# A planned decoder trunk: new constants in the plan's model of loads and product changes, and two filler products in place of eleven

## The chip, the cores and the metric

The kernel runs on one core of one Trainium2 chip. The metric is the device time of one execution in microseconds (us), the median of several runs. The core has five engines that run their own instruction streams and meet only at semaphores: TensorE (PE, with its weight loads shown as PEld), VectorE (DVE), ScalarE (ACT), GpSimd (POOL) and SyncE (SP, which here does nothing but issue DMAs).

## The reference

The program is a decoder trunk of two layers over a sequence of 512 tokens with 1024 features, all in float32. What one layer computes, cut to its core:

```python
mod = c_silu @ w_ada + b_ada
shift, scale, gate = jnp.split(mod, 3, axis=-1)
u = rms_norm(x, norm_g) * (1 + scale[:, None]) + shift[:, None]
z = u @ w_in                       # 18 column groups: q, k, v, gates of three mixers, indexer, merge gates
ya = dsa_attention(...)     * silu(ag)   # indexer scores, top 128 keys, softmax attention
yb = swa_sinks_attention(...) * silu(bg) # window of 128 keys, sinks
yc = stick_breaking_attention(...) * silu(cg)
merged = sigmoid(ma) * (ya @ w_br_a) + sigmoid(mb) * (yb @ w_br_b) + sigmoid(mc) * (yc @ w_br_c)
x = x + gate[:, None] * (merged @ w_out)
```

After both layers a final `rms_norm` is taken. Each mixer has eight heads of 64 features.

## The kernel before

**Staging.** Activations lie with features on the partitions, as 8 tiles of 128 x 512. Nearly every product is made in three parts: weights and activations are each split into a high part and a low part (`whi`, `wlo`; `uh`, `ul`), and TensorE adds high x high, high x low and low x high in one PSUM bank. Weights come as 128 x 512 pieces through four buffers (`wstage`); a cast makes `whi`, a subtraction makes `wlo`, on whichever of ACT, DVE and POOL the plan picks.

A layer runs through five parts: `first_phase` (L923: seven column tiles over all eight `u` tiles, so that it can begin as soon as `u` tile 0 stands), `v_phase` (L975: the value columns), a long middle in which the three mixers, the remaining column tiles and the branch products are woven together, and `out_phase` (L1360). In the mixers, each pair of heads goes through score products, softmax or stick-breaking on ACT and DVE, 128 x 128 transposes (`softmax_tr`, L1218), and then `softmax_pv` (L1244): eight products whose stationary operand is only 64 columns wide, four key blocks (j) for each of two heads (e), written in the program in the order e0 j0, e1 j0, e0 j1, e1 j1 and so on. The two heads write the two halves of the same PSUM bank. These are the half-width products; the model calls them mode "c". Another sort, mode "r", has only 64 rows (`low_parts`, L1073, seven products in one item). Full products are "m", transposes "t".

**The plan.** No instruction is issued where the program names it. `Recorder.add` (L280) records every operation with its data dependencies and, where several engines could do it, the alternatives. `price` (L313) gives each alternative a cost (how long it holds its engine) and a lag (when its result stands). `forward` (L385) then plays the whole program: at each step it takes, over all engines, the instruction that can start first, and among those that can start at the same time on an engine the one with the most urgent priority. `latest` (L506) works back from the end and gives each instruction the latest time at which it may start; that is the priority of the next round. There are five rounds (L253), the first with program order as priority, and the round with the earliest modelled end is issued (`emit`, L545; every profile row therefore has line L555, or L553 for the seven products of mode "r"). The chip runs each engine's instructions strictly in the order that the plan wrote down, whatever the real times are. The model's times decide only that order, the choice of engine and the choice of buffer.

Loads are modelled as one queue: a DMA lands at `max(at + 1.9, dma_free)` plus its bytes over a rate, and `dma_free` is the landing of the one before. A product costs more when the mode changes from or to "c" or "r".

**The start of the program** (`start`, L1436) is where the second part of the edit lies. It issues eight products on a constant (`WARM`), computes `silu(c)` and spreads it over the partitions (`csr`, two products), loads x in two halves of 256 tokens (`norm`, L1459: loads, squares on ACT, products with a constant that sum over the features, then `rstd_of`: a logarithm and an exponential on ACT). The scale and shift of `u` tile j come from 512 KB loads into `Y` (`ada_load`, L724) and two long multiply-and-sum operations on DVE (`ada_first`, L729). Between these stand filler products: `busy` (L1469) multiplies a constant with the first 128 columns of a tile into a bank that nobody reads, so that a filler waits for its tile and then occupies TensorE.

Of the kernel before, what the change touches and what calls it, by code (L numbers as in the profile page):

```python
# [249 lines left out]
class Recorder:  # L250
# [62 lines left out]
    def price(self, x, engine, op, args, kw):  # L313

        y = Way()
        y.op, y.args, y.kw, y.mode, y.port = op, args, kw, None, False
        o = x.writes[0] if x.writes else None
        if op == "preload_act_table_set":
            y.cost = y.lag = 1.3
            return y  # L320
        if op == "dma_start":
            n = 1
            for d in (o or x.reads[0]).shape:
                n *= d
            y.cost, y.lag, y.mode = 0.35 if engine == "SP" else 0.1, n * 4 / 365e3, "dma"
            return y
        n = 1
        for d in o.shape[1:]:
            n *= d
        from_psum = any(v.tile.pool.name[:3] == "ps_" for v in x.reads)  # L330
        if engine == "PE":
            if op == "pairs":
                w = [q[2].shape[-1] for q in args]
                c, y.mode = 0.095 + sum(max(0.112, 0.4375e-3 * v + 0.007) for v in w[::2]), "r"
                y.cost, y.lag = c, c + self.PIPE
            elif op == "transpose":
                c, y.mode = 0.109, "t"
                y.cost, y.lag = c, c + self.PIPE
            elif args[1].shape[-1] == 64:
                c, y.mode = 4 * n / 2.4e3 / 2 + 0.03, "c"  # L340
                y.cost, y.lag = c, 2 * c + self.PIPE
            else:
                rhs, y.mode = args[2], "m"
                c = 4 * n / 2.4e3 + 0.01 if rhs.dtype == F32 else 0.06 if rhs.dtype == BF16 else 0.4375e-3 * n + 0.007
                y.cost, y.lag = c, c + self.PIPE
            return y
        accum = "accum_out" in kw
        if engine == "ACT":
            b = 0.1 if isinstance(kw.get("bias"), View) or isinstance(kw.get("scale"), View) else 0.0
            c = 0.2 + 0.82e-3 * n + (b if not accum else 0.08) - (0.03 if from_psum else 0)  # L350
        elif engine == "DVE":
            y.port = not from_psum and op not in ("max", "match_replace", "memset", "reciprocal")
            if op == "tensor_tensor_scan":
                c = 1.21
            elif op == "max":
                c = 0.15 + 1.05e-3 * args[1].shape[-1]
            elif op == "match_replace":
                c = 0.145 + 1.05e-3 * args[2].shape[-1]
            elif n <= 16:
                c = 0.2 + (0.1 if accum else 0)  # L360
            elif op == "tensor_tensor_reduce":
                c = 0.147 + 1.05e-3 * n
            elif from_psum:
                c = 0.147 + 1.05e-3 * n + (0.08 if accum else 0)
            elif op in ("tensor_scalar", "tensor_copy"):
                c = 0.2 + 0.45e-3 * n if op == "tensor_scalar" else 0.15 + 0.5e-3 * n
            elif op == "memset":
                c = 0.1 + 0.6e-3 * n
            else:
                c = 0.15 + 1.05e-3 * n + (0.08 if accum else 0)  # L370
        else:
            y.port = n > 16
            if op == "memset":
                c = 0.12 if n < 16 else 0.52
            elif op == "tensor_copy":
                c = 0.2 + 0.82e-3 * n
            elif op == "tensor_scalar":
                c = 0.2 + 2.8e-3 * n
            else:
                c = 0.1 + 2.35e-3 * n  # L380
        y.cost = y.lag = c
        return y


    def forward(self):  # L385
        E = {e: {"free": 0.0, "mode": None, "ready": {}, "pend": []} for e in self.real}
        port = dma_free = 0.0
        waiting = {}
        for x in self.list:
            x.left, x.est, x.bound, x.taken = len(x.preds), 0.0, len(x.tiles), False  # L390
# [8 lines left out]
        def offer(x):  # L399
            if x.left == 0 and x.bound == 0:  # L400
                for e in x.alts:
                    heapq.heappush(E[e]["pend"], (x.est, x.i))
# [20 lines left out]
        while len(out) < len(self.list):  # L423
            best = None
            for name, e in E.items():
                free, pend, ready = e["free"], e["pend"], e["ready"]
                while pend and pend[0][0] <= free + 1e-9:
                    i = heapq.heappop(pend)[1]
                    ready[i] = self.list[i]
                mine = None  # L430
                for i in list(ready):
                    x = ready[i]
                    if x.taken:
                        del ready[i]
                        continue
                    y = x.alts[name]
                    at = max(free, port) if y.port else free
                    if len(x.alts) > 1 and self.elsewhere(x, name, at, E, port):
                        continue
                    key = (at, x.prio, i)  # L440
                    if mine is None or key < mine:
                        mine = key
                if mine is None or mine[0] > free + 1e-9:
                    while pend and self.list[pend[0][1]].taken:
                        heapq.heappop(pend)
                    if pend:
                        est, i = pend[0]
                        x = self.list[i]
                        at = max(est, port) if x.alts[name].port else est
                        key = (at, x.prio, i)  # L450
                        if (mine is None or key < mine) and not (len(x.alts) > 1 and self.elsewhere(x, name, at, E, port)):
                            mine = key
                        elif mine is None:
                            mine = None
                if mine is not None:
                    asked = max(free, self.list[mine[2]].est)
                    if best is None or (mine[0], asked, mine) < best[:3]:
                        best = (mine[0], asked, mine, name)
            assert best is not None, "no instruction may go"
            (at, _, i), name = best[2:]  # L460
            e, x = E[name], self.list[i]
            y = x.alts[name]
            x.taken, x.engine = True, name
            e["ready"].pop(i, None)
            hold = y.cost
            if name == "PE":
                if e["mode"] is not None and y.mode != e["mode"]:
                    hold += 0.095 if {"c", "r"} & {y.mode, e["mode"]} else 0.0
                e["mode"] = y.mode
            x.start, x.hold = at, hold  # L470
            e["free"] = at + hold
            if y.port:
                port = at + hold
            if y.mode == "dma":
                x.end = dma_free = max(at + 1.9, dma_free) + y.lag
            else:
                x.end = at + y.lag + (hold - y.cost)
            out.append(x)
            for s in x.succs:
                s.est = max(s.est, x.end + self.between(x, s))  # L480
                s.left -= 1
                offer(s)
            for t in x.tiles:
                t.users -= 1
                t.done = max(t.done, x.end + self.CROSS)
                if t.users == 0:
                    heapq.heappush(t.pool.free, (t.done, t.slot))
                    give(t.pool)
# [89 lines left out]
def trunk(ctx, tc, xT, vecs, w_ss, w_gt, w_first, w_t, w_v, w_br, w_o, rope, consts, out):  # L578
# [7 lines left out]
    PE, ACT, DVE, POOL, SP = (rec.engine(e) for e in ("PE", "ACT", "DVE", "POOL", "SP"))  # L586

    def fixed(name, shape, dt=F32):
        return rec.fixed(const.tile(shape, dt, name=name))
# [13 lines left out]
    def mm(o, lhsT, rhs, start, stop=True):  # L603
        PE.matmul(o, lhsT, rhs, start=start, stop=stop, skip_group_check=True)
# [831 lines left out]
    def start():  # L1436
# [4 lines left out]
        e = fixed("e", [P, 8], F32)  # L1441
# [14 lines left out]
        x = st["x"] = [xx[k // 4][:, k % 4] for k in range(KT)]  # L1456
# [12 lines left out]
        def busy(n, v):  # L1469
            for _ in range(n):  # L1470
                mm(st["warm"][:, :P], f(nones), v[:, :P], True)
# [1 line left out]
        norm(HALVES[0])  # L1473
        ada_load(0)
        ch.load(1)
        busy(3, ch.raw[0][0])
        busy(4, ch.raw[1][0])
        ada_first(0)
        for k in (0, 1):
            times_rstd(x[k], HALVES[0])  # L1480
            busy(2, x[k])
        make_u(0, 0, x[0], HALVES[0])
        norm(HALVES[1])
        ada_load(1)
# [48 lines left out]
    ch = Chunks(seq)  # L1533
# [72 lines left out]
```

## Time and profile before

| what | us |
|---|---|
| median of three runs (lowest, highest) | 1219.49 (1219.07, 1220.74) |
| the profiled execution | 1219.63 |
| its span, first to last instruction | 1217.8 |
| TensorE busy in the span | 1200.4 |
| VectorE busy | 962.1 |
| ScalarE busy | 556.3 |
| GpSimd busy | 264.3 |

Rows of the profile name an operation by engine, instruction, output and inputs. "xN" counts records: a product with plain float32 operands leaves two records, one with split operands leaves one. In a row of the timeline the first number is the start in us from the span's beginning, the second how long the row lasts, and the bracket gives the engine's idle time before it and what ended that. TensorE products overlap: the time that one takes from the next is the distance between starts, which is shorter than its duration.

### The profile page before, as it was taken

Reading aid. Unit: us, or ns where it says so; the run is one execution under the profiler, and the core shown is the slowest. Engines: PE = TensorE matmul, PEld = TensorE weight load, DVE = VectorE, ACT = ScalarE, POOL = GpSimd, SP = SyncE. Lnnn points to the kernel's source line nnn. Section 1 sums busy time; section 2 is a strip of 40 time slices with the busy share of each in tenths; the row PEclk is TensorE's granted clock in tenths of the full one; section 3 lists DMA queues with packets and bytes.
Section 4 is the critical chain, followed back from the end, with each engine's and each line's share of the span. In section 5 each row is a group of like instructions: output and inputs, shape, how many; then the busy total and the mean of one; then the engine's idle time right before and its main releaser. Section 6 shows DMA issues by size and latency. Waiting matters only on the chain.

```text
span 1217.8 us, 17816 instructions
## 1 busy us (share of the span) xinstructions
PE 1200.4 (99%) x6006; PEld 976.3 (80%) x6006; DVE 962.1 (79%) x2106; ACT 556.3 (46%) x1166; POOL 264.3 (22%) x290
## 2 busy tenths in 40 slices
PE   9999999999999999999999999999999999999997
PEld 8899777788777887688898987777878878877886
DVE  6867999899879888686476699989996887667754
ACT  6623677454445532632143157664534654234222
POOL 1200446432111110011200015454220110100120
PEclk9999999999999999999999999999999999999999
DMA  9644222344334455245533432223442324323343
GB/s 318 231 119 124 83 70 84 104 114 117 109 96 122 129 146 150 69 130 145 171 109 98 133 95 78 85 69 116 121 122 70 96 80 120 95 64 79 93 123 102
DMA packets 81915, 139.40 MB, mean 114 GB/s; under 512 B 10016, under 2 KB 22560, under 8 KB 81824
## 3 DMA queue, kind: packets, MB, share of 16 engines
q1 hardware_dynamic: 80672, 136.17, 38.6%
q10 hardware_dynamic: 1152, 2.10, 0.5%
q8 instruction: 47, 0.77, 0.3%
q14 instruction: 44, 0.36, 0.1%
HBM read 125.39 MB, written 4.19 MB: 106 GB/s over the span
## 4 chain that ended last, share of the span: by engine, by line
PE 89%; DVE 4%; SPq 2%; DMA 2%; ACT 1%; issue 1%; POOL 1%; DVEq 0%; ACTq 0%; POOLq 0%
PE ps_z L555 67%; PE ps_s L555 22%; SPq L555 2%; PE ps_s L553 1%; DMA m<-zs 1%; DVE t L555 1%; DVE Q L555 1%; DVE m L555 1%; DMA wstage<-in_w_first 1%; DMA wstage<-in_w_t 0%; ACT t L555 0%; POOL KH L555 0%; DVE score L555 0%; DVE zc L555 0%; DVE den L555 0%
## 5 line engine op out<-in xcount | busy, mean ns | idle before, releaser
L555 PE MATMUL ps_z<-uh,whi 128*128 128x512 f32 (+1 forms) x908 | 359.1, 397 | 2.2 <-DVE xm L555 2.2
L555 PE MATMUL ps_z<-uh,wlo 128*128 128x512 f32 (+1 forms) x908 | 356.0, 393 | 0.0
L555 PE MATMUL ps_z<-ul,whi 128*128 128x512 f32 (+1 forms) x908 | 355.8, 392 | 0.0
L555 POOL TENSOR_TENSOR wlo<-wstage,whi 128x512 fp32r<-128x512 f32 (+1 forms) x131 | 175.1, 1339 | 662.8 <-DVE whi L555 312.0
L555 PEld LDWEIGHTS ps_z<-uh,whi 128*128 128x128 f32 x908 | 170.3, 188 | 41.9 <-DVE xm L555 3.1
L555 PEld LDWEIGHTS ps_z<-uh,wlo 128*128 128x128 f32 x908 | 170.5, 188 | 38.7 <-issue 1.8
L555 PEld LDWEIGHTS ps_z<-ul,whi 128*128 128x128 f32 x908 | 170.6, 188 | 35.9 <-issue 1.0
L555 DVE TENSOR_TENSOR wlo<-wstage,whi 128x512 fp32r<-128x512 f32 (+2 forms) x241 | 158.2, 660 | 12.8 <-ACT whi L555 3.6
L555 DVE CAST whi<-wstage 128x512 fp32r<-128x512 f32 (+2 forms) x181 | 74.7, 412 | 112.9 <-PE ps_z L555 94.5
L555 ACT CAST whi<-wstage 128x512 fp32r<-128x512 f32 (+2 forms) x141 | 83.4, 596 | 169.7 <-PE ps_z L555 125.9
L555 PE MATMUL ps_z<-Y,whi 128*128 128x512 f32 x384 | 121.7, 396 | 0.0
L555 ACT ACTIVATE e<-ps_z 128x512 f32<-128x512 f32 x68 | 40.2, 592 | 131.7 <-PE ps_z L555 131.4
L555 PEld LDWEIGHTS ps_z<-Y,whi 128*128 128x128 f32 x384 | 71.7, 188 | 17.0
L555 ACT ACTIVATE e<-e 128x512 f32<-128x512 f32 x96 | 60.6, 633 | 39.9 <-DVE e L555 39.1
L555 PE MATMUL ps_z<-Y,wlo 128*128 128x512 f32 x192 | 75.8, 395 | 0.0
L555 ACT ACTIVATE t<-t 128x512 f32<-128x512 f32 x120 | 71.8, 628 | 6.1 <-DVE t L555 2.7
L555 ACT ACTIVATE t<-t,nm 128x256 f32<-128x256 f32 (+3 forms) x128 | 65.2, 511 | 18.0 <-DVE nm L555 17.9
L555 PEld LDWEIGHTS ps_s<-small,t 128*128 128x128 f32 x432 | 50.3, 140 | 13.3 <-ACT t L555 2.9
L555 PE MATMUL ps_s<-small,t 128*128 128x128 f32 x432 | 58.6, 274 | 1.8 <-ACT t L555 1.3
L555 POOL CAST whi<-wstage 128x512 fp32r<-128x512 f32 (+2 forms) x50 | 31.2, 623 | 134.0 <-PE ps_z L555 63.1
L555 DVE SCALAR_TENSOR_TENSOR wstage<-wstage,csr 128x512 f32<-128x512 f32 x64 | 47.3, 740 | 9.4 <-DMA wstage<-in_w_ss 6.7
L555 DVE MAX8 m<-score 128x8 f32<-128x256 f32 (+2 forms) x96 | 53.2, 555 | 1.0
(208 smaller groups left out, 2066.8 us busy)
## 6 DMA issues: line engine op xcount, KB each, us to landing
wstage<-in_w_t SPq DMA_DIRECT2D x212, 256.0 KB, 2.7
wstage<-in_w_v SPq DMA_DIRECT2D x48, 182.0 KB, 2.4
Y<-in_w_ss SPq DMA_DIRECT2D x16, 512.0 KB, 6.7
m<-zs SPq DMA_DIRECT2D x128, 64.0 KB, 2.0
wstage<-in_w_gt SPq DMA_DIRECT2D x32, 256.0 KB, 2.7
wstage<-in_w_ss SPq DMA_DIRECT2D x32, 256.0 KB, 2.7
wstage<-in_w_o SPq DMA_DIRECT2D x32, 256.0 KB, 2.7
wstage<-in_w_first SPq DMA_DIRECT2D x16, 256.0 KB, 3.1
```

The source lines that it names most:

```text
L553: self.real[engine].matmul(*[real(a) for a in q], start=False, stop=True, skip_group_check=True)
L555: getattr(self.real[engine], y.op)(*[real(a) for a in y.args], **{k: real(v) for k, v in y.kw.items()})
```

## The change

Four edits. (1) The modelled rate of loads goes from 365e3 to 350e3 bytes per us. (2) The modelled load queue is free from 2.9 us on and not from 0. (3) A change of mode that involves "c" or "r" is charged 0.19 us when the next product is a full one and 0.12 us otherwise; before, it was 0.095 us either way. Changes between "m" and "t" stay free. (4) Of the filler products, two on the first weight piece stay; five on the first and second weight pieces (net) and four on x tiles 0 and 1 go. No other instruction is added or removed, but all of the plan is made anew, so any engine's order can differ anywhere.

```diff
-            y.cost, y.lag, y.mode = 0.35 if engine == "SP" else 0.1, n * 4 / 365e3, "dma"
+            y.cost, y.lag, y.mode = 0.35 if engine == "SP" else 0.1, n * 4 / 350e3, "dma"
...
-        port = dma_free = 0.0
+        port, dma_free = 0.0, 2.9
...
                 if e["mode"] is not None and y.mode != e["mode"]:
-                    hold += 0.095 if {"c", "r"} & {y.mode, e["mode"]} else 0.0
+                    if {"c", "r"} & {y.mode, e["mode"]}:
+                        hold += 0.19 if y.mode == "m" else 0.12
...
         norm(HALVES[0])
         ada_load(0)
         ch.load(1)
-        busy(3, ch.raw[0][0])
-        busy(4, ch.raw[1][0])
+        busy(2, ch.raw[0][0])
         ada_first(0)
         for k in (0, 1):
             times_rstd(x[k], HALVES[0])
-            busy(2, x[k])
         make_u(0, 0, x[0], HALVES[0])
```

## The prediction

> **What bounds the kernel now.** I read the page first: the span, and the busy time of the engines.
>
> ```profile
> span 1217.8 us, 17816 instructions
> PE 1200.4 (99%) x6006; PEld 976.3 (80%) x6006; DVE 962.1 (79%) x2106; ACT 556.3 (46%) x1166; POOL 264.3 (22%) x290
> ```
>
> TensorE is idle for 17.4 of 1217.8 us. So the time can move in three ways only: idle time of TensorE, products that are not needed, and products that cost more than they must. The view by stretches says where the idle time is.
>
> ```profile
> 21.00:56.00 35.00, 35.00 (x181) 29.69 (x182) 30.48 (x55) 21.08 (x42) 6.72 (x8) 1.00 0.80 273
> 56.00:1208.00 1152.00, 1145.71 (x5726) 930.39 (x5725) 916.50 (x2016) 521.20 (x1097) 255.80 (x273) 1.00 0.37 106
> ```
>
> The columns after the length are busy times of PE, PEld, DVE, ACT and POOL. From 21 to 56 us TensorE never rests; from 56 to 1208 us it rests 6.3 us in 1152. The remaining 11 us are before 21 us and after 1208 us. The tail is not touched by the edits except through the plan.
>
> The start, TensorE's timeline:
>
> ```profile
> 1.03 3.78 PE L555 MATMUL ps_s<-nones 128*128 128x128 f32 x16 [1.03 <-DVE epst L555]
> ...
> 7.57 2.75 PE L555 MATMUL ps_s<-t,nones 128*128 128x256 f32 x12
> 11.82 1.83 PE L555 MATMUL ps_s<-wstage,nones 128*128 128x128 f32 x14 [1.50 <-DMA wstage<-in_w_first]
> 13.81 1.16 PE L555 MATMUL ps_s<-vc,nones 128*128 128x128 f32 x8 [0.16 <-DVE vc L555]
> 14.81 1.03 PE L555 MATMUL ps_s<-t,nones 128*128 128x256 f32 x4
> ...
> 20.95 0.39 PE L555 MATMUL ps_z<-uh,whi 128*128 128x256 f32 x1
> ```
>
> The rows with wstage and vc as inputs are the eleven fillers (two records each): seven from 11.82 us, four from 13.81 us. From 14.81 us on everything is real work, without a gap except a fraction at 20.95 us. A real product moved ahead of 14.81 us is therefore worth its full time, until the next thing that is late.
>
> **The fillers (edit 4).** A filler takes 1.83 / 7 = 0.26 us. The five that go at 11.82 us stand where TensorE would otherwise wait for data that ACT has yet to make, so I price them at nothing; the cover is that wait. The four on x start at 13.81 us and push the next real row to 14.81 us: 1.00 us straight ahead of the dense run. Is that real work ready? ACT's timeline:
>
> ```profile
> 11.80 0.62 ACT L555 CAST whi<-wstage 128x512 fp32r<-128x512 f32 x1 [0.40 <-DMA wstage<-in_w_first]
> ...
> 13.36 0.62 ACT L555 ACTIVATE t<-vc 128x512 f32<-128x512 f32 x1
> 13.88 0.59 ACT L555 ACTIVATE uh<-vc,mods,amul 128x256 fp32r<-128x256 f32 x1
> ```
>
> The first square of the second half of x (t) stands at 13.36 + 0.62 = 13.98 us, `uh` of tile 0 at 14.47 us. So real products can start about 14.0 us, 0.8 us sooner, and there are enough of them. The upper bound of the gain is 1.2 us, with real work ready where the last wstage filler ends now, at 11.82 + 1.83 = 13.65 us; the lower bound is 0, because of what is late next: at 20.95 us TensorE takes up `u` tile 1, which ACT can make only when its scale (`amul`) stands. That comes from DVE:
>
> ```profile
> 19.18 0.08 DVE L555 DVE_READ_ACCUMULATOR Y<-Y,csr 128x1 f32 x1
> 19.37 0.69 DVE L555 TENSOR_TENSOR wlo<-wstage,whi 128x512 fp32r<-128x512 f32 x1
> 19.98 0.27 DVE L555 TENSOR_SCALAR amul<-dot,small,gb 128x1 f32<-128x1 f32 x1
> ```
>
> The sum that `amul` needs is there at 19.26 us; a weight split goes ahead of it. Without that, `amul` would stand near 19.5 us and `uh`, with the 0.59 us of the row at 13.88 us, at 20.1 us. Between 19.9 us (when TensorE would now be through) and then, it has the second half of `u` tile 0, if the plan has made that by then. I take 0.9 us, nearer the upper end than the lower, because the next two edits act on exactly this order.
>
> **The loads (edits 1 and 2)** cost nothing themselves; they change which instruction the plan puts first on an engine that must wait in order. By the code, the model has the first weight piece landing at 1.9 + 2.47 MB / 0.365 = 8.7 us (112 KB of vectors, 1 MB of x, 1 MB of `Y`, 256 KB), the changed one at 2.9 + 2.47 / 0.350 = 10.0 us. SP's first issue is at 0.7 us of the span, so the cast at 11.80 us, which waited for that landing, says 11.1 us in the model's count: 2.4 us too early before, 1.1 us now. How the rate fits is in the mean over the stretch that follows, last column in GB/s:
>
> ```profile
> 11.80:35.80 24.00, 23.79 (x153) 21.59 (x154) 21.52 (x41) 15.52 (x32) 2.73 (x4) 1.00 1.01 354
> ```
>
> 354 GB/s is close to the new 350. What a load that is planned too early does is seen at 35.81 us on ACT:
>
> ```profile
> 35.81 0.62 ACT L555 CAST whi<-wstage 128x512 fp32r<-128x512 f32 x1 [4.23 <-DMA wstage<-in_w_first]
> ...
> 37.36 0.82 ACT L555 ACTIVATE uh<-va,mods,amul 128x512 fp32r<-128x512 f32 x1
> ...
> 38.40 0.62 PE L555 MATMUL ps_z<-uh,whi 128*128 128x512 f32 x2
> ```
>
> ACT sits 4.23 us before a cast, with `uh` of tile 4 queued behind it; `uh` is ready at 38.18 us and TensorE uses it at 38.40 us. With only 0.2 us to spare there, a gain of 0.9 us at the start would be lost again at tile 4 if ACT's order stayed. With the later landings the plan has a reason to put `uh` first. So these edits are worth nothing by themselves (the wait is hidden today) and carry the gain of the fillers past 38 us; without them the sum is 0.2 us and not 0.9. After 56 us loads run at some 100 GB/s and the rate decides little.
>
> **The charge (edit 3)** adds no instruction either. What a change really costs, and what a block of half-width products costs whole and torn:
>
> ```profile
> 167.45 0.39 PE L555 MATMUL ps_z<-ul,whi 128*128 128x512 f32 x1
> 167.68 0.40 PE L555 MATMUL ps_z<-uh,wlo 128*128 128x512 f32 x1
> 168.00 2.37 PE L555 MATMUL ps_s<-t,vc 128*64 128x512 f32 x16
> ...
> 217.48 2.37 PE L555 MATMUL ps_s<-t,vc 128*64 128x512 f32 x8
> ...
> 220.20 2.15 PE L555 MATMUL ps_s<-t,vc 128*64 128x512 f32 x6
> ...
> 223.18 0.43 PE L555 MATMUL ps_s<-t,vc 128*64 128x128 f32 x2
> ```
>
> The same eight products take 2.37 us in one run and 2.37 + 2.15 + 0.43 = 4.95 us in three, since the two heads no longer go in turn: a torn block costs 2.6 us more. Of that the change of mode is little, 0.09 us each way (0.32 us between the starts at 167.68 and 168.00 where 0.23 is usual). Nine of the 24 blocks are torn so today, by the timeline. The charge comes after a choice and not before it, so it doesn't make the plan hold a block back until all its inputs are there: it only makes the modelled TensorE slower by 0.025 + 0.095 us at each of some 54 visits. Its direct effect I price at 0, with one block either way, -2.6 to +2.6 us, as the bounds.
>
> How much a new deal does is shown by the same work in other surroundings, the busy time of TensorE (second column) on half-width products in the first and the second layer, first for the stick-breaking mixer, then for the windowed one:
>
> ```profile
> 120.00:560.00 440.00, 12.98 (x64) 5.82 (x64) 3.09 (x5) 1.85 (x3) 1.00 0.39 111
> 724.00:1160.00 436.00, 12.98 (x64) 5.82 (x64) 3.50 (x6) 1.14 (x2) 1.00 0.33 92
> 120.00:560.00 440.00, 10.67 (x64) 6.60 (x64) 0.00 (x0) 0.00 (x0) 1.00 0.39 111
> 724.00:1160.00 436.00, 9.27 (x64) 6.37 (x64) 0.00 (x0) 0.00 (x0) 1.00 0.33 92
> ```
>
> The one mixer agrees to 0.01 us, the other differs by 1.4 us. So a new deal tears or mends a block or two, not ten.
>
> **The sum**, from the profiled execution's 1219.63 us (span 1217.8, 1.8 around it; 0.14 above the median shown): fillers at 11.82 us 0, fillers on x -0.9, loads 0, charge 0: 1218.7, and 0.14 less for the median: 1218.6 us.
>
> **The rivals.** (A) Torn blocks mend. For it: nine torn blocks and a slower modelled TensorE, so that a block's later inputs stand when it begins. Against it: the tear happens at the first input's arrival, which no edit moves. Two net blocks mended give 1218.6 - 2 x 2.6 = 1213.4 us. (B) The other sign: blocks tear. 15 of 24 are not torn now, and ACT and DVE get another order everywhere; from two net torn blocks on the sum turns, 1218.6 + 5.2 = 1223.8 us. For it: the windowed mixer's 1.4 us between the layers shows that a block can fall either way; against it: the stick-breaking mixer's eight blocks cost the same in both. (C) Nothing arrives: `u` tile 1 still comes at 20.9 us or tile 4 at 38.2 us, since the modelled first landing is still 1.1 us early, and the fillers only turn into idle time: 1219.4 us. (D) The clock. The rows of the very end:
>
> ```profile
> 1210.00:1211.00 1.00, 0.62 (x3) 0.19 (x2) 0.00 (x0) 0.34 (x1) 0.00 (x0) 1.00 0.00 0
> 1214.00:1215.00 1.00, 0.00 (x0) 0.00 (x0) 0.28 (x1) 0.00 (x0) 0.00 (x0) 0.50 1.03 338
> ```
>
> The third column from the end is the granted clock: after TensorE ran dry it fell to half. The start has run at half pace too: 16 records in 3.78 us (0.24 each) in the row at 1.03 us, 14 of the same size in 1.83 us (0.13 each) at 11.82 us; the row at 7.57 us, of double size, is at full pace already (2.75 / 12 = 0.23). So a slow spell lasts some 4 us, and one that began at 14 us would cost 4 x 0.5 = 2.0 us of the dense run: 1218.6 + 2.0 = 1220.6 us. After the edit TensorE does two fillers, 0.5 us, between about 10.3 us and 14.0 us, about as little as in the stretch before the fall at the end. Against it: the 1.5 us of idleness that the row at 11.82 us shows has not done it. [...]
>
> **How the numbers follow.** Chances: the forecast 0.43, A 0.22, B 0.13, C 0.13, D 0.09. Some 0.2% (2.4 us) is what a measurement of this kernel can tell from no change, so faster means under 1217.1 us and slower over 1221.9 us. The forecast's own range, with one block's 2.6 us either way, is 1216.0 to 1221.2 us; about 0.13 of its 0.43 lies under 1217.1 us. With A that makes 0.35 for faster. Slower is B and a hundredth of the rest, 0.14. C, D and the rest of the forecast leave 0.51 for no difference. The range reaches to A on one side and not quite to B on the other: 1213.4 to 1222.2 us.
>
> **What would show it right or wrong.** Right: four records on wstage and none on vc among the fillers; the first square's products near 14.0 us instead of 14.81; `uh` of tile 4 made ahead of the cast that waits for its load; TensorE still without a gap from 21 to 56 us, and the span shorter by 0.9 us. The first step is wrong if an idle gap of up to 1 us appears before `u` tile 1 or 4; the second if ACT still waits some 4 us in front of `uh` of tile 4. The price of the charge is wrong if the 128*64 rows of the two layers add up to something over 2.6 us away from today's. D shows as 128x256 products at 0.23 us from start to start after 14 us. The whole prediction is wrong if the time moves by over 3 us: then blocks were mended or torn in numbers, and the start is a side matter.

## The result and the profile after

The changed kernel takes 1233.27 us, the median of four runs (1231.58 to 1235.23), against 1219.28 us for the kernel before on the same chip: a ratio of 1.0111, 95% interval 1.0097 to 1.0125. It is 14 us slower. The forecast was 1218.6 us, the range went to 1222.2. The profiled execution is the fastest of the four (1231.58 us, mean granted clock 0.994; the others had 0.991 or 0.992), so the trace shows 12 of the 14 us, and by those clocks the others lost some 2 to 3 us more to slow clock, at places that no trace shows.

The page of the changed kernel, first the span and the engines:

```profile
span 1229.7 us, 17826 instructions
PE 1201.8 (98%) x5988; PEld 976.7 (79%) x5988; DVE 968.7 (79%) x2108; ACT 555.1 (45%) x1156; POOL 261.3 (21%) x298
```

The span grew by 11.9 us. TensorE's idle time went from 17.4 to 1229.7 - 1201.8 = 27.9 us, its busy time from 1200.4 to 1201.8 us although nine fillers are gone. By this first count the loss is waiting. The view by stretches says where, and that a part of it hides in "busy". The columns are those of the prediction; the third from the end is the granted clock. First the changed kernel, then two rows of the kernel before:

```profile
21.00:56.00 35.00, 34.84 (x180) 29.41 (x181) 30.57 (x55) 19.48 (x38) 3.83 (x9) 1.00 0.82 276
56.00:1208.00 1152.00, 1137.40 (x5634) 921.32 (x5633) 916.67 (x2002) 517.84 (x1084) 253.00 (x278) 1.00 0.36 105
200.00:260.00 60.00, 56.18 (x279) 43.96 (x279) 54.45 (x115) 33.34 (x71) 26.67 (x29) 0.97 0.32 89
800.00:860.00 60.00, 53.35 (x256) 41.64 (x257) 51.59 (x109) 32.86 (x70) 24.87 (x27) 0.94 0.31 88
```

```profile
200.00:260.00 60.00, 58.79 (x290) 45.42 (x289) 55.66 (x128) 33.01 (x71) 32.25 (x31) 1.00 0.35 95
800.00:860.00 60.00, 58.20 (x283) 44.57 (x283) 55.73 (x130) 29.86 (x65) 33.81 (x33) 1.00 0.33 97
```

The start is not the place: from 21 to 56 us TensorE loses 0.16 us. The two stretches of 60 us, one in each layer, are the hand-over from the stick-breaking mixer to the windowed one. There TensorE now rests 3.8 and 6.7 us where it rested 1.2 and 1.8: 7.5 us more. And there alone, between 21 and 1208 us, the clock is not whole. The two places, close up, in the changed kernel:

```profile
241.00:245.00 4.00, 3.70 (x10) 2.97 (x11) 3.60 (x14) 4.00 (x16) 0.00 (x0) 0.57 0.24 66
842.00:849.00 7.00, 5.98 (x15) 4.71 (x16) 6.60 (x22) 6.10 (x22) 0.10 (x1) 0.51 0.11 34
```

TensorE counts as busy there and does half its work: 4.0 x 0.43 + 7.0 x 0.49 = 5.1 us lost, inside "busy". The trace's clock record has half clock for 3.41 us from 241.23 on and for 6.83 us from 841.98 on. 7.5 of waiting at the two places and 5.1 of half clock make 12.6 us; small gains and losses in the rest of the run balance it to 11.9.

What stands before each slow stretch, in TensorE's timeline (the bracket is the idle time and what ended it):

```profile
235.65 0.39 PE L556 MATMUL ps_z<-Y,wlo 128*128 128x512 f32 x1
...
238.45 0.40 PE L556 MATMUL ps_z<-Y,wlo 128*128 128x512 f32 x1
241.30 0.77 PE L556 MATMUL ps_z<-uh,whi 128*128 128x512 f32 x1 [2.46 <-ACT t L556]
...
843.02 0.76 PE L556 MATMUL ps_z<-uh,whi 128*128 128x512 f32 x1 [3.99 <-ACT t L556]
```

The product that waits opens a new group of column tiles and needs a free bank (one of the PSUM areas in which TensorE leaves its sums). The trace names ACT as releaser; the bank it gets is the one that held the first branch product, and VectorE empties that (`xm<-ps_z`). VectorE in the same stretch:

```profile
232.65 1.46 DVE L556 CAST Q<-zc 64x512 fp32r<-64x512 f32 x1
234.14 2.36 DVE L556 TENSOR_TENSOR Q<-zc,Q 64x512 fp32r<-64x512 f32 x2
236.52 0.42 DVE L556 CUSTOM_DVE_ANT_0 t<-ps_s,cb 128x256 f32<-128x256 f32 x1
...
238.67 0.78 DVE L556 TENSOR_SCALAR nm<-mx,sk 128x4 f32<-128x4 f32 x2
239.35 0.55 DVE L556 MAX8 m<-score 128x8 f32<-128x384 f32 x1
...
240.01 0.54 DVE L556 MATCH_REPLACE8 score<-m,score 128x384 f32<-128x384 f32 x1
240.47 0.68 DVE L556 TENSOR_TENSOR xm<-ps_z,sm 128x512 f32<-128x512 f32 x1
```

The bank's last product is the first row of TensorE's timeline above; it ended at 236.04 us. VectorE comes to it at 240.47, behind three operations on 64 partitions (3.8 us), seven reductions, two short products and a step of the top-k search. At 241.15 the bank is free, and TensorE goes on at 241.30. That the releaser is `xm` and not ACT was put to the test below.

### The profile page after: what moved, and what is told of

Same layout as the page of the kernel before. It is cut to its first block, busy times and chain, and to the rows that moved or that the text cites. A ratio compares the mean times of both kernels' runs of the same rounds, so it can differ in the third digit from the quotient of the medians.

```text
span 1229.7 us, 17826 instructions
## 1 busy us (share of the span) xinstructions
PE 1201.8 (98%) x5988; PEld 976.7 (79%) x5988; DVE 968.7 (79%) x2108; ACT 555.1 (45%) x1156; POOL 261.3 (21%) x298
## 3 DMA queue, kind: packets, MB, share of 16 engines
q10 hardware_dynamic: 1152, 2.10, 0.5%
## 4 chain that ended last, share of the span: by engine, by line
PE 89%; DVE 5%; ACT 2%; DMA 2%; SPq 1%; issue 1%; DVEq 0%; ACTq 0%
PE ps_z L556 67%; PE ps_s L556 21%; SPq L556 1%; DVE t L556 1%; DMA m<-zs 1%; DVE Q L556 1%; PE ps_s L554 1%; DVE KH L556 1%; ACT t L556 1%; DMA wstage<-in_w_first 1%; DVE zc L556 0%; DVE m L556 0%; ACT e L556 0%; ACT whi L556 0%; DVE wlo L556 0%
## 5 line engine op out<-in xcount | busy, mean ns | idle before, releaser
L556 POOL TENSOR_TENSOR wlo<-wstage,whi 128x512 fp32r<-128x512 f32 (+1 forms) x142 | 186.7, 1315 | 635.4 <-DVE whi L556 282.7
L556 ACT CAST whi<-wstage 128x512 fp32r<-128x512 f32 (+2 forms) x147 | 87.4, 597 | 166.6 <-PE ps_z L556 117.3
L556 DVE TENSOR_TENSOR wlo<-wstage,whi 128x512 fp32r<-128x512 f32 (+2 forms) x230 | 149.8, 656 | 12.9 <-ACT whi L556 3.0
L556 DVE CAST whi<-wstage 128x512 fp32r<-128x512 f32 (+2 forms) x170 | 69.8, 411 | 111.8 <-PE ps_z L556 95.4
L556 DVE MATCH_REPLACE8 score<-m,score 128x256 f32<-128x256 f32 (+2 forms) x96 | 52.1, 543 | 0.0
```

What stands on the lines that cost most here:

```text
L556: getattr(self.real[engine], y.op)(*[real(a) for a in y.args], **{k: real(v) for k, v in y.kw.items()})
```

## The experiments

All times are medians, and every ratio is against the kernel before on the same chip. Each profile shows one execution, which can lie some us beside the median. Gaps in the expectations are counted from start to start, less the usual distance of two products; they are some 0.2 us longer than the brackets of the timeline.

**One edit at a time.** The charge alone (edit 3):

```diff
-                    hold += 0.095 if {"c", "r"} & {y.mode, e["mode"]} else 0.0
+                    if {"c", "r"} & {y.mode, e["mode"]}:
+                        hold += 0.19 if y.mode == "m" else 0.12
```

> The kernel before with edit 3 alone (0.19 us when the next product is a full one, else 0.12 us; loads and fillers as before). Theory R (a new deal): the time is lost because the plan writes another order for VectorE where the stick-breaking mixer hands over to the windowed one, so that TensorE runs dry there in both layers and its clock falls; this edit alone moves that order (the plan puts half-partition operations between the last scans, none before), so 1225 to 1236 us. Theory S (the start): the time is lost through the missing fillers and the moved loads; then 1217 to 1221 us here.

Measured: 1220.85 us, ratio 1.0009 (1.0000 to 1.0018). Theory R is out for the charge alone; the time lies in theory S's range, which the next two runs do not support.

The model of the loads alone (edits 1 and 2):

```diff
-            ... n * 4 / 365e3, "dma"
+            ... n * 4 / 350e3, "dma"
-        port = dma_free = 0.0
+        port, dma_free = 0.0, 2.9
```

> The kernel before with edits 1 and 2 alone (350e3 bytes per us, queue free from 2.9 us). Theory R: VectorE's order at the hand-over changes by one half-partition operation only, so 1218 to 1224 us, the start no more than 1 us different. Theory S: several us slower, 1223 to 1230 us.

Measured: 1210.84 us, ratio 0.9927 (0.9911 to 0.9944). It is faster than either kernel; neither theory had this. Half of the gain is a mended block in each layer, rival A of the prediction. The row at 217.48 us, which was torn into three rows before, in this run:

```profile
217.48 2.60 PE L555 MATMUL ps_s<-t,vc 128*64 128x512 f32 x16
```

All half-width products together take 67.9 us of TensorE and not 72.2: 4.3 of the 8.5 us by which the span shrinks. Another 2.7 us are idle time (14.7 us and not 17.4).

The fillers alone (edit 4; but for the fillers, and a few products of the start, every engine has the order of the kernel before):

```diff
-        busy(3, ch.raw[0][0])
-        busy(4, ch.raw[1][0])
+        busy(2, ch.raw[0][0])
...
-            busy(2, x[k])
```

> The kernel before with edit 4 alone (two fillers of eleven). In the plan the fillers stand in idle time, and every other instruction keeps its place. Theory R: 1218.4 to 1220.4 us. Theory S, or a clock that falls in the gap at 10 to 14 us: 1221 to 1226 us.

Measured: 1220.58 us, ratio 1.0006 (0.9996 to 1.0015). That is between the two ranges. What the second one named is seen in the view by stretches, at a price of 1 us: the gap that the fillers leave is followed by a slow clock:

```profile
10.00:14.00 4.00, 0.86 (x5) 0.52 (x4) 3.83 (x7) 2.29 (x6) 0.51 (x1) 1.00 1.08 368
14.00:18.00 4.00, 3.59 (x13) 3.24 (x14) 2.33 (x5) 2.69 (x6) 0.00 (x0) 0.57 1.06 385
```

A charge that differs from the old one by one hundredth, to see how much any new order moves:

```diff
-                    hold += 0.095 if {"c", "r"} & {y.mode, e["mode"]} else 0.0
+                    if {"c", "r"} & {y.mode, e["mode"]}:
+                        hold += 0.096 if y.mode == "m" else 0.096
```

> The kernel before with a charge of 0.096 us in place of 0.095 us for each change of mode that involves half-width products, nothing else. Theory R: what counts is that the order is dealt anew and not by how much the charge grows; the plan puts four half-partition operations between the last scans as it does with all four edits, so 1225 to 1236 us. Rival C (the size of the charge: the modelled TensorE is too slow by 0.12 us per visit): no difference, 1218 to 1221 us.

Measured: 1220.37 us, ratio 1.0011 (1.0001 to 1.0020). What follows from the four: the single edits give +1.2, -8.8 and +1.0 us against 1219.6, which add up to -6.6; together they give +14.0. So no edit has a price of its own that could be summed. The theory that the half-partition subtractions (VectorE operations on 64 of the 128 partitions) between the last scans are enough to lose the time fell, because the run with 0.096 has them there and loses 0.8 us.

**Two edits at a time.** Without the charge (edits 1, 2 and 4 of the diffs above):

```diff
-            ... n * 4 / 365e3, "dma"
+            ... n * 4 / 350e3, "dma"
-        port = dma_free = 0.0
+        port, dma_free = 0.0, 2.9
-        busy(3, ch.raw[0][0])
...
+        busy(2, ch.raw[0][0])
```

> Edits 1, 2 and 4 together, the charge as before. Theory I (an interaction of the loads with the charge: only the plan made under both puts VectorE's work at the hand-over from the stick-breaking to the windowed mixer in the bad order): the order of the loads-alone run with a start like that of the fillers-alone run, 1210.8 + 1.0 = 1211.8 us, at most 1214. Theory F (the loads need the fillers' cover, and the two together lose): over 1222 us.

Measured: 1219.56 us, ratio 0.9998 (0.9988 to 1.0009). Neither theory had this.

Without the fillers' edit (1, 2 and 3):

```diff
-            ... n * 4 / 365e3, "dma"
+            ... n * 4 / 350e3, "dma"
-        port = dma_free = 0.0
+        port, dma_free = 0.0, 2.9
-                    hold += 0.095 if {"c", "r"} & {y.mode, e["mode"]} else 0.0
+                    if {"c", "r"} & {y.mode, e["mode"]}:
+                        hold += 0.19 if y.mode == "m" else 0.12
```

> Edits 1, 2 and 3 together, all eleven fillers kept. Theory I: all of the loss is there, 1231 to 1234 us, with idle gaps over 2.5 us near 238 and 838 us and the granted clock at half behind them. Theory F: under 1222 us.

Measured: 1225.95 us, ratio 1.0055 (1.0040 to 1.0070), with the gaps at both hand-overs and half clock behind them (TensorE busy for 0.72 us from 835 to 839 us, then a granted clock of 0.61 to 843 us; a clock of 0.97 in the mean from 200 to 260 us), as theory I expected, but under its range and 7 us less than with all four edits. So beside the new model of the loads, taking the fillers away costs 7 to 9 us (1219.56 - 1210.84 and 1233.27 - 1225.95), while by itself it costs 1.

In each of these pairs both kernels have the same order on VectorE, ScalarE, GpSimd and SyncE past the first 70 us, so these 7 to 9 us are not lost by another order but by other timing within the same one. The first pair is the clearest case. Up to 784 us the trace without the charge lags the one with the loads alone by 0.20 us. Then, VectorE and GpSimd with the loads alone:

```profile
818.69 0.69 DVE L555 TENSOR_TENSOR m<-m,rt 128x512 f32<-128x512 f32 x1 [1.21 <-DMA m<-zs]
821.30 0.68 DVE L555 TENSOR_TENSOR Q<-zc,Q 64x512 fp32r<-64x512 f32 x1
822.26 1.43 DVE L555 TENSOR_TENSOR Q<-zc,Q 64x512 fp32r<-64x512 f32 x1 [0.28 <-ACT Q L555]
826.77 0.68 DVE L555 TENSOR_TENSOR xm<-ps_z,sm 128x512 f32<-128x512 f32 x1
...
821.67 3.19 POOL L555 TENSOR_TENSOR wlo<-wstage,whi 128x512 fp32r<-128x512 f32 x2 [0.40 <-ACT whi L555]
...
827.60 0.47 PE L555 MATMUL ps_z<-uh,whi 128*128 128x512 f32 x1 [0.84 <-DVE xm L555]
```

The same instructions without the charge, with the fillers' edit:

```profile
821.07 0.69 DVE L555 TENSOR_TENSOR m<-m,rt 128x512 f32<-128x512 f32 x1 [2.38 <-DMA m<-zs]
823.67 4.29 DVE L555 TENSOR_TENSOR Q<-zc,Q 64x512 fp32r<-64x512 f32 x2
831.59 0.67 DVE L555 TENSOR_TENSOR xm<-ps_z,sm 128x512 f32<-128x512 f32 x1
...
823.61 2.53 POOL L555 TENSOR_TENSOR wlo<-wstage,whi 128x512 fp32r<-128x512 f32 x2
826.11 1.48 POOL L555 TENSOR_SCALAR e<-e 128x512 f32<-128x512 f32 x1
...
832.41 0.77 PE L555 MATMUL ps_z<-uh,whi 128*128 128x512 f32 x1 [4.45 <-DVE xm L555]
```

Small transfers for the rotation (`m<-zs`) land late twice, by 1.0 us at 794 us and by 1.2 us more here, so `m` starts 2.4 us later. By then GpSimd has its next input waiting and works without a pause, and it began 0.06 us before VectorE's subtraction. That subtraction, the first of the two in the row of 4.29 us, takes 3.59 us where it took 0.68. The bank is emptied 4.8 us later, TensorE's gap is 4.45 us and not 0.84, and 3.4 us of half clock follow (granted clock 0.58 from 832 to 836 us). The same order costs 6 us more in these two traces, and this chain is where they part: late transfers, then VectorE a fraction of a microsecond behind GpSimd. (Why the transfers came late isn't settled. The medians differ by 8.7 us; the profiled execution, 1217.33 us, is one of the faster ones of the run without the charge.)

**The gap and the clock, each by itself.** The changed kernel's plan, with VectorE's operation that empties the bank taken ahead of reductions, in both layers. `behind(ids, i)` takes the instructions `ids` out of the finished order and puts them directly behind instruction `i`:

```diff
+        behind((1965, 1899, 1900, 1901, 1902), 1964)   # xm0, then four reductions, behind the bank's last product
+        behind((6644, 6578, 6579, 6580, 6581), 6643)
```

> The changed kernel's plan with one move in each layer: VectorE's product that empties the bank of the first branch group (xm0) goes ahead of four or five reductions, as soon as the bank's last product is issued. Nothing else is moved. Theory H (the late bank makes the gaps, and the gaps make the clock fall): the gaps at 238 us (2.6) and 838 us (4.2, of which about 1 us stays since the subtractions ahead of it are slow) go, and so do the stretches at half clock (1.7 + 3.4): 1233.3 - 2.6 - 3.2 - 5.1 = 1222.4 us, 1221 to 1225. Theory L (VectorE is late anyway, and what TensorE waits for is only passed on): 1229 us or more, with a new gap behind.

Measured: 1226.45 us, ratio 1.0066 (1.0046 to 1.0085): 6.8 us less than the changed kernel, of 11 expected. Both gaps before the bank are gone; so the bank was what TensorE waited for. Two waits of the second layer in this run, the first at the scans of the stick-breaking mixer, the second, new, before the transposes of the windowed mixer:

```profile
811.26 0.41 PE L567 MATMUL ps_s<-small,t 128*128 128x128 f32 x2 [2.12 <-DVE t L567]
...
844.26 0.98 PE L567 MATMUL ps_s<-small,t 128*128 128x128 f32 x7 [1.60 <-DVE t L567]
```

The gap at the scans was there before the move as well (2.66 us, at 813 us), but now it is this one that the clock answers:

```profile
811.00:814.50 3.50, 3.24 (x12) 2.75 (x13) 3.43 (x6) 1.26 (x2) 2.34 (x4) 0.60 0.37 137
```

So theory H holds for the gap and theory L for a part of the time: some of the wait is passed on, since VectorE is late in this whole stretch.

The changed kernel's plan, and TensorE kept busy in the two gaps (the products add zero to a bank; `self.zero` is a tile that GpSimd fills with zeros beforehand):

```diff
+                for _ in range({1982: 9, 6661: 15}.get(x.i, 0)):
+                    self.real[engine].matmul(real(y.args[0]), self.zero, real(y.args[2]), start=False, stop=True, ...)
```

> The changed kernel's plan, and in the two gaps TensorE is kept busy: 9 products with a zero stationary tile behind the last branch product before the gap at 238 us, 15 before the one at 838 us; they add zero to a bank that is read later. The gaps stay. Theory H: the clock stays up, 1233.3 - 5.1 = 1228.2 us, granted clock .998, and the runs lie closer together. If the fall of the clock has another cause than idle time: 1233 us and clock .991 to .994 as in the changed kernel.

Measured: 1227.06 us, ratio 1.0062 (1.0047 to 1.0077), 6.2 us less than the changed kernel. The same two stretches as above:

```profile
241.00:245.00 4.00, 3.64 (x16) 2.74 (x15) 3.59 (x13) 4.00 (x17) 0.06 (x1) 1.00 0.20 70
842.00:849.00 7.00, 7.00 (x40) 5.94 (x39) 5.83 (x18) 5.25 (x15) 3.15 (x3) 1.00 0.26 75
```

The clock stays whole, and in the seven us 26 full products and 14 records of transposes go where 15 full products went. The real work waits as long as before, and 6 us come back: the fall of the clock follows from TensorE's idleness, and it is nearly half of the loss. The two runs overlap, since without the gaps there is no fall behind them: their 6.8 and 6.2 us can't be added, and the two changes together were not tried.

Bank and scans first: as the bank-first run, and the four subtractions for KH moved behind the last scan as well:

```diff
+        behind((1633, 1634, 1637, 1638), 1692)
+        behind((6312, 6313, 6316, 6317), 6371)
```

> The changed kernel's plan with the bank-first move of the run before in both layers, and besides the four half-partition subtractions (KH) of each layer moved from between the last stick-breaking scans to behind the last one. Theory H (VectorE's order at the hand-over makes the gaps): the gaps at 214 us (1.5) and 809 us (2.3) and the 1.7 us of half clock behind the latter go too: 1226.45 - 5.5 = 1221 us, 1219 to 1224. Theory L (what those operations make is needed just then, so TensorE waits for it instead): 1226 us or more.

Measured: 1225.62 us, ratio 1.0050 (1.0034 to 1.0067). The time lies outside theory H's range. The gaps at the scans go and others come up behind; 0.8 us is within the spread of the executions (1222.4 to 1230.7). This part of theory H fell: which of VectorE's operations is late is only exchanged.

The bank first in the two plans with the new model of the loads, first without the charge and the fillers' edit, then with the latter:

```diff
+        behind((1974, 1909, 1910, 1911, 1912), 1973)   # edits 1 and 2
+        behind((6653, 6588, 6589, 6590, 6591), 6652)
...
+        behind((1965, 1900, 1901, 1902, 1903), 1964)   # edits 1, 2 and 4
+        behind((6644, 6579, 6580, 6581, 6582), 6643)
```

> Edits 1 and 2 alone, with the bank-first move in both layers. Theory H: the two gaps of that run, 0.6 us at 236 and 1.0 us at 826, go: 1210.8 - 1.6 = 1209.2 us. Theory L: 1210.8 us, the gap turns up at the next bank.

> Edits 1, 2 and 4, with the bank-first move in both layers. By the traces this plan is that of the loads alone but for the first 60 instructions, and its loss (8.7 us) lies in one gap of 4.6 us at 828 us, where VectorE's subtraction for Q took 3.59 us and not 0.68 beside GpSimd's three operations without a pause, and in half the clock behind it. Theory P (the wait for GpSimd holds VectorE up, and the bank is queued behind it): with the bank ahead of four reductions the gap shrinks from 4.6 to some 1 us and the clock stays up: 1219.6 - 3.6 - 1.7 = 1214.3 us, 1212 to 1216, though the long subtraction may stay. Theory F (the missing fillers lose it elsewhere): 1218 us or more.

Measured: 1211.17 us (ratio 0.9930, 0.9915 to 0.9945) and 1215.47 us (0.9962, 0.9948 to 0.9977). Small gaps, of under 1 us, are passed on: nothing gained, theory L. The gap of 4.45 us isn't: 4.1 us gained, of 5.3 expected, theory P.

**The price of a torn block.** Edits 1 and 2, and the two heads' products of a key block as one item of the plan, which can't be parted and which the model prices as two single ones:

```diff
-                    mm(y[64 * e:64 * e + 64, ...], ..., j == 0)
+                    duo.append((y[64 * e:64 * e + 64, ...], ..., j == 0))
+                rec.add({"PE": ("duo", tuple(duo), {})})
```

> Edits 1 and 2 alone, and the two heads' half-width products of each key block are one item of the plan, so that they always stand side by side and no block can be torn; the plan is made anew. If the price of a torn block is what the prediction read (some 2.6 us each), 16.3 us of over-cost go: 1210.8 - 16.3 = 1194.5 us, 1190 to 1201 with what a new order may add or take. If TensorE only turns the over-cost into waiting for the later head's input: 1206 to 1216 us.

Measured: 1205.79 us, ratio 0.9887 (0.9872 to 0.9902). The engines' line of the page with the loads alone, and with whole pairs:

```profile
PE 1194.7 (99%) x6006; PEld 975.9 (81%) x6006; DVE 958.2 (79%) x2102; ACT 552.7 (46%) x1154; POOL 274.0 (23%) x306
...
PE ps_z L555 <- DVE xm L555: 1.3, 2, 0.8
```

```profile
PE 1179.0 (98%) x6006; PEld 967.5 (80%) x6006; DVE 972.4 (81%) x2096; ACT 558.8 (46%) x1164; POOL 269.3 (22%) x302
...
PE ps_z L562 <- DVE xm L562: 5.2, 2, 2.6
```

TensorE's busy time falls by 15.7 us, of 16.3 expected, and all of it in the half-width products (52.1 us and not 67.9), so the over-cost of torn blocks was read rightly. But only 5 us arrive in the median. Between the two profiled executions the span falls by 6.8 us (1209.3 to 1202.5), so 8.9 us turn into idle time. Before the bank TensorE waits 5.2 us in place of 1.3 (the second rows, from the view of waits: us in total, times, longest). With the bank first in this plan:

```diff
+        behind((1958, 1894, 1895), 1957)
+        behind((6589, 6525, 6526), 6588)
```

> The loads alone with whole pairs, and the bank-first move in both layers: its gaps of 2.8 us at 234 and at 822 us stand before the same bank. Theory H (the gap goes with the late bank): 1205.8 - 5.5 = 1200.3 us, 1198 to 1202.5. Theory L (VectorE is late in this stretch anyway, and TensorE waits at a later bank, as with the loads alone): 1204 us or more.

Measured: 1201.89 us, ratio 0.9858 (0.9841 to 0.9874), 3.9 us less, by theory H. It is the best kernel of these runs: 17.7 us under the one before.

**Is it the values, or one order out of many?** Neighbouring rates:

```diff
-            ... n * 4 / 350e3, "dma"
+            ... n * 4 / 351e3, "dma"   # all four edits; then edits 1 and 2 alone
+            ... n * 4 / 352e3, "dma"   # all four edits
```

> The changed kernel with the modelled rate 351e3 instead of 350e3, nothing else. Theory V (the loss belongs to the values): 1231 to 1236 us. Theory O (it belongs to one order out of many that lie close together in the model): anywhere from 1212 to 1234 us, more likely than not under 1229.

> The changed kernel with the modelled rate 352e3. Theory V: 1231 to 1236 us. Theory O: 1212 to 1234 us, and not the time of the run with 351e3.

> Edits 1 and 2 alone with the modelled rate 351e3. Theory V: 1209 to 1213 us. Theory O: over 1213 us, up to 1225.

Measured: 1219.93 us (ratio 1.0001, 0.9991 to 1.0011), 1217.98 us (0.9986, 0.9977 to 0.9995) and 1219.95 us (1.0005, 0.9995 to 1.0014). With a rate 0.3% higher the whole loss of 14 us is gone, and so is the whole gain of 8.8 us with the loads alone. Theory O: neither the loss nor the gain belongs to the values of the change. They belong to the order that the plan happens to write for 350e3, and to the timing that it meets, and the four edits with a rate of 352e3, 351e3 or 350e3 are worth -1.6, +0.3 or +14 us. With 351e3 and all four edits, the two stretches around the hand-over:

```profile
200.00:260.00 60.00, 58.59 (x307) 46.66 (x307) 56.54 (x127) 32.36 (x70) 28.32 (x34) 1.00 0.36 99
800.00:860.00 60.00, 57.88 (x294) 45.88 (x293) 57.78 (x136) 31.36 (x69) 30.48 (x36) 1.00 0.34 93
```

TensorE rests 1.4 and 2.1 us where it rested 3.8 and 6.7, with the clock whole. VectorE is busier there than in the changed kernel (56.5 and 57.8 us; 54.5 and 51.6): what counts is which operation comes first and how long it is held up, not how full VectorE is.

## Why the prediction was wrong, point by point

**The step that failed** is the sentence on the charge, "So a new deal tears or mends a block or two, not ten", and the bound of 2.6 us either way that was put on it. By its letter the sentence held: in the plans counted here, at most two net blocks were mended or torn. But it took torn blocks as the only thing that another order can change, and put TensorE's waiting in the middle of the run, and the clock behind it, at nothing. In the changed kernel torn blocks hardly changed. The windows by layer that the prediction quoted, for the changed kernel, in the same order:

```profile
120.00:560.00 440.00, 11.96 (x64) 5.61 (x64) 3.09 (x5) 1.84 (x3) 1.00 0.38 109
724.00:1160.00 436.00, 11.96 (x64) 5.60 (x64) 3.52 (x6) 1.24 (x2) 0.99 0.31 90
120.00:560.00 440.00, 10.81 (x64) 6.00 (x64) 0.00 (x0) 0.00 (x0) 1.00 0.38 109
724.00:1160.00 436.00, 10.59 (x64) 6.09 (x64) 0.00 (x0) 0.00 (x0) 0.99 0.31 90
```

They add up to 45.3 us against 45.9. What changed is how late VectorE is at the hand-over, and what half clock that brings: 12.6 us in the trace. Taking away the wait for the bank gave 6.8 us back, keeping TensorE busy in the gaps 6.2. The row that the prediction should have quoted is in the view of TensorE's waits of the kernel before:

```profile
PE ps_z L555 <- DVE xm L555: 2.2, 2, 1.2
```

Two waits of over a microsecond in the middle of a run that otherwise has none, both before the same bank, one per layer, with VectorE busy 55.7 of 60 us around each. "TensorE rests 6.3 us in 1152" was read as little to win; it was to be read as the place where VectorE is already late, and where a few operations more ahead of that bank can go straight into the time.

**The loads** "cost nothing themselves": wrong. Alone they gave -8.8 us, half of it in mended blocks, and +0.4 at 351e3. "The rate decides little" after 56 us is true of when loads land and false of which order is written. The part about `uh` came true. ACT in the changed kernel:

```profile
36.30 0.82 ACT L556 ACTIVATE uh<-va,mods,amul 128x512 fp32r<-128x512 f32 x1
...
37.91 0.61 ACT L556 CAST whi<-wstage 128x512 fp32r<-128x512 f32 x1
```

The wait of 4.23 us before the cast is gone and `uh` of tile 4 is made ahead of it, a microsecond sooner. TensorE uses it at 38.45 us, 0.05 later than before: nothing was gained by it.

**The fillers**: the two on `wstage` stay, none on x, as said. The gain of 0.9 us did not come. TensorE in the changed kernel:

```profile
11.76 0.71 PE L556 MATMUL ps_s<-wstage,nones 128*128 128x128 f32 x4 [1.12 <-DMA wstage<-in_w_first]
14.35 1.97 PE L556 MATMUL ps_s<-t,nones 128*128 128x256 f32 x8 [1.88 <-DVE vc L556]
...
21.02 0.50 PE L556 MATMUL ps_z<-uh,whi 128*128 128x256 f32 x2 [0.47 <-ACT uh L556]
```

The squares' products start at 14.35 us, not at 14.0; the 0.46 us won against 14.81 are lost again before `u` tile 1, as rival C had it (0.13), at 21.02 instead of 20.95. The size of the term was off by all of it; the thing that is late next was named rightly.

**Rival D** (the clock, 0.09) had the mechanism and the wrong place. At the start it was seen in the run with the fillers' edit alone (0.57 from 14 to 18 us), in the bank-first run of edits 1, 2 and 4 (half clock for 3.41 us from 13.82 on) and in the run with 352e3 (6.83 us from 14.24 on): in three traces with the fillers' edit. It isn't in the trace of the changed kernel, and whether its three slower executions had it is not known. With all eleven fillers the granted clock of the first 21 us is 1.00 in five traces (the kernel before, the charge alone, the loads alone, the two together, the charge of 0.096); the mean clock of the other four is 0.998, that of the kernel before. At the hand-over the same mechanism cost 5.1 us, and no part of the prediction looked for it there. The two stretches of half clock at the hand-over lasted 3.41 and 6.83 us, where the prediction's estimate for a slow spell was some 4 us.

**Rivals A and B** (blocks mend or tear) are out as causes of the result: counted block by block against whole ones, nine blocks with over 1 us of over-cost became ten, and the over-cost of all 24 went from 20.3 to 19.6 us. Rival A did come true with the loads alone, where two blocks mended, although the prediction held that no edit moves what tears a block. The price was right in sum (15.7 us of 16.3 in the run with whole pairs); the block that the prediction quotes is the dearest, others cost 1.6 to 1.9 us more than whole ones. "Over 3 us: then blocks were mended or torn in numbers" was the wrong conclusion.

**The range** was drawn from one mechanism. Orders from models that differ by a hundredth or less in one constant differed by up to 15 us (350e3 and 352e3 with all four edits), and all plans made from these constants ran from 1211 to 1233 us; a range for a change that makes the plan anew would have had to be that wide.

What isn't settled: why the transfers for the rotation land a microsecond later in one run than in the other; how the 7 us between the changed kernel and the one that keeps all fillers divide into single waits; where the other half of the loss stays when the bank is freed first; and what edits 3 and 4 do together, which was not tried.

## What to carry to other kernels

Where a planner writes the order from a model, a changed constant is first of all another draw: compare several neighbouring values before believing a gain or a loss, and price it from the places where the bottleneck engine already waits, not from the constant's meaning. Where a buffer that the bottleneck engine needs stands in the queue of a second, nearly full engine (VectorE here, 55.7 of 60 us), late operations there turn into idle time, and an idle time of 2.1 to 4.0 us cost nearly as much again in clock in three places of these traces (1.7 us behind gaps of 2.12 and 2.46 us, 3.4 us behind 3.99; nothing behind one of 2.66). Where such a wait is long, put what frees a bank ahead of what merely uses one, and make inseparable what costs double when it is parted: these two gave 9 us on top of the loads' order. Whether they give as much on the order of another constant was not tried.

## What the runs showed of the hardware that was not expected

**How short a gap lowers the clock.** An idle time of 2.12 us at 809 us did it in the bank-first run (0.60 in the row above); one of 2.66 us at 813 us did not in the changed kernel:

```profile
815.68 0.41 PE L556 MATMUL ps_s<-small,t 128*128 128x128 f32 x2 [2.66 <-DVE t L556]
```

In the changed kernel's clock record, full and half clock take turns in stretches of 235.52, 3.41, 597.33, 6.83 and 375.47 us from 5.71 us on: 69, 1, 175, 2 and 110 times 3.413 us. Laid out in windows of that length from the first full clock on, the shorter gap falls whole into one, the longer into two. The window with the gap of 2.12 us in the bank-first run, and the emptier of the two in the changed kernel:

```profile
808.32:811.73 3.41, 1.29 (x8) 0.81 (x7) 3.37 (x4) 1.28 (x3) 1.00 (x1) 1.00 0.54 131
811.26:814.67 3.41, 1.76 (x10) 1.11 (x8) 3.35 (x4) 2.08 (x5) 1.34 (x1) 1.00 0.23 58
```

TensorE is busy for 38% of the first window and 52% of the second. Half clock follows the first (0.60 from 811 to 814.5 us, above) and not the second. Laid out so in the traces of the kernel before and of the changed kernel, four windows at full clock are followed by half clock, with TensorE busy for 14, 21, 30 and 33% (the changed kernel's from 838.57 us, the kernel before's from 1209.92 us, the changed kernel's from 237.82 and from 1220.86 us); the emptiest of the others has 47% (the changed kernel's from 12.54 us). So in these windows the share of busy time parts the two outcomes, and the length of the gap doesn't: 2.12 us was enough, 2.66 us was not. In the changed kernel full clock came back behind windows of 98% and 100% (from 241.23 and 845.39 us) and not behind one of 70% (from 841.98 us, in which TensorE still waits for a microsecond): there the fall lasts two windows.

**How long VectorE can be held up.** A subtraction on 64 partitions with both inputs in SBUF takes 0.68 us, and 3.59 us when it begins just behind the first of three GpSimd operations that follow each other without a pause (the rows at 821.30 and 823.67 us); in the changed kernel's trace 47 of 64 such subtractions begin beside no GpSimd operation and none of these takes over 0.69 us; of the 17 that begin beside one, 14 take 1.2 to 1.8 us. VectorE's reductions that read PSUM take 0.42 us all the while. How long such a subtraction takes beside GpSimd differs: in the row at 822.26 us it took 1.43 us and ended while GpSimd was still at the pair of 3.19 us, in the row at 823.67 us it took 3.59 us and ended when the third of three was under way. What decides that, no run here shows.
